# A hybrid decoder layer: narrow products between wide ones, log decays sent as rows, and the order of the key convolutions

## The chip, the core and the metric

The kernel runs on one core of a Trainium2 chip. TensorE (PE in the profile) multiplies, VectorE (DVE), ScalarE (ACT) and GpSimd (POOL) work elementwise, and SyncE (SP) issues all the DMAs. Each engine takes its instructions in the order written for it and waits at semaphores for the others. The metric is device time in microseconds (us), the median over runs, of one launch with batch 1, 1024 tokens and a model width of 1024, all in float32.

## The reference, cut to what matters

The layer is an RMS norm, one input projection, two mixers side by side (a gated delta rule with 4 heads of width 128, and a dilated window attention with 8 heads of width 64), an output projection, and an MLP with a short convolution. The change touches the norm, the gates `b_a`, `a_a`, and the keys of the delta rule:

```
h = rmsnorm(x, norm1_w);  proj = h @ w_in
qkv_a = silu(causal_dwconv(qkv_a, conv_qkv_w))       # width 4, q, k, v of 4 heads
qa = l2norm(qa) * 128 ** -0.5;  ka = l2norm(ka)
beta = sigmoid(b_a)
g = -exp(a_log) * softplus(a_a + dt_bias)            # log decay, one per token and head
gc = cumsum(g over the chunk)
diff = gc[..., :, None] - gc[..., None, :]
dec_incl = where(incl, exp(diff), 0)
lmat = where(strict, dec_incl, 0) * (k @ k^T) * beta
sol = triangular_solve(I + lmat, [v, exp(gc) * k])
```

Then a scan over the chunks, the attention, `x + concat(A, B) @ w_out`, the MLP, and a final norm.

## The kernel before, in words

**Products.** A projection of float32 data is made from three fp32r products of split operands (high by high, low by high, high by low: `mm3`). One such product has 128x128 weights and 512 moving columns; below it is a "wide" product. A column block of the input projection (128 columns of the weights) has two halves of 512 tokens, and each half takes 8 slices of the width x 3 = 24 wide products, collected in one PSUM bank of 512.

**Order of the work.** PE's order is fixed by a planner (class `Weave`): each part of the kernel is a generator that issues products and yields the time until it wants to go on. The planner always lets the ready generator with the lowest level go on, counting time by its own estimates for each engine (`ve`, `ac`, `po_`, `sy`, and the `us` given to `mm`). `norms()` has level 0, `gates()` 1, the key, query and value preparations 3 and 4, `first()` and `dense()` 9, so that wide products fill what the others leave. A token keeps the products on PE in that order. The orders of DVE, ACT, POOL and SP come from a scheduler that runs over dependencies and a cost model of its own; `after()` adds an order without a semaphore.

**Start.** While `xT` arrives in 8 slices, `first()` multiplies each slice with the weights of keys 0 to 2 into six banks (tags `hf`, `asc`, `ch`, two each): 8 x 18 = 144 wide products. Meanwhile `acc` collects the sum of squares. `norms()` reduces `acc` with 8 products of one column (`ones<-acc`), takes the power on POOL, and spreads the result over the partitions by 8 transposes into `rstdB`. `gates()` multiplies the raw slices with an 8 column weight (`xt,wba`, 16 products), turns it back with 8 products of 8 columns (`sel,barow`), computes `g`, and makes the cumulative sum `gc` by one product with a triangle `tri`. These are the narrow products.

**Keys.** `dense()` then runs the column blocks in the order `DENSE`: key 3, two blocks of attention, then q and v by head, and so on. Its two halves alternate in the two `hf` banks. Every bank is emptied by DVE, which multiplies it by `rstdB` into `xr` (`scaled`). `conv_silu` convolves: a copy on ACT, three multiply-adds `d = 1, 2, 3` on DVE, tanh on ACT, and a last multiply-add on DVE. `kprep(h)` then makes from `gc` the decay matrix `dec` of head h: 8 transposes of `gc`, broadcast, into `atr` banks (`ident,gc`), 8 ACT instructions of 128x128 that subtract, a mask on POOL, and an exp on ACT. It transposes the keys (8 products `ident,kT`; ACT copies them to `ktok` and squares them, `sq`, with a sum), multiplies keys by keys (8 products `kT<-kT` into `atr` banks), and DVE scales the result into `um`. The `atr` tag has two banks, so a third user waits until ACT or DVE is done with the first. After the fourth key, `um` goes through DRAM to `forward_sub`, a chain of 62 small DVE instructions, then follow `merge`, the scan `chain`, attention, the output projection and the MLP.

**Slots.** `xr` of key 3 takes a slot of tag `ev`, of which there are two.

```
A("xr", "ev")                       # through scaled(): keys 0, 1 and 3; key 2 takes "qa"
pg = yield from next_bank("atr")    # kprep: bank for the broadcast decays
```

Of the kernel before, what the change touches and what calls it, by code (L numbers as in the profile page):

```python
# [10 lines left out]
OP = mybir.AluOpType  # L11
# [9 lines left out]
FT = 22  # L21
NEG = -1.0e30
EPS = 1e-6
SLOTS = {"kT": 2, "kU": 2, "dv": 2, "dw": 2, "kt": 4, "uy": 5, "qa": 4, "ev": 2, "go": 2, "Xa": 7, "Xb": 9}
# [110 lines left out]
def hybrid_layer(tc, I, out):  # L135
# [35 lines left out]

    def after(inst, anchor):
        tc.add_manual_dep(inst.ins, anchor.ins.name, order, reason="keeps a slot free until it is needed")

# [14 lines left out]
    def split(src, hi, lo):  # L189
        ac.activation(hi, src, AF.Copy)  # L190
        ve.tensor_tensor(lo, src, hi.bitcast(F32), op=OP.subtract)

# [21 lines left out]
    mixer = dp.tile([8, P, S], F32, name="mixer")  # L214
    mdram = dp.tile([H, 32, 1024], F32, name="mdram")
    xdram = dp.tile([H, 32, 1024], F32, name="xdram")
    xtdram = dp.tile([H, 32, 1024], F32, name="xtdram")
# [34 lines left out]
    for k in range(KT):  # L252
# [8 lines left out]
        if k == 0:  # L261
            sy.dma_start(wst[:, 0, :], I["w0"][0, :, 0])
            for h in range(2):
                sy.dma_start(xt[:, half(h)], I["xT"][:P, half(h)])
            sy.dma_start(wst[:, 1, :], I["w0"][0, :, 1])
            split(wst[:, 0, :], whi[:, 0, :], wlo[:, 0, :])
            for h in range(2):
                split_x(xt, 0, half(h))
            split(wst[:, 1, :], whi[:, 1, :], wlo[:, 1, :])
        else:  # L270
            if k % 2 == 0:
                sy.dma_start(wst, I["w0"][k // 2])
            sy.dma_start(xt, I["xT"][k * P:(k + 1) * P, :])
            if k % 2 == 0:
                split(wst, whi, wlo)
            split_x(xt, k, slice(0, S))
        sq = A("sq", "qa")
        ac.activation(sq, xt, AF.Square)
        if k == 0:
            sq0 = sq  # L280
        elif k == 1:
            ve.tensor_tensor(acc, sq0, sq, op=OP.add)
        else:
            ve.tensor_tensor(acc, acc, sq, op=OP.add)

# [41 lines left out]
    def norms():  # L327
        yield wv.need(acc, slack=10.0)
        ssp = yield from next_bank("atr", acc)
        for c in range(NCH):  # L330
            mm(ssp[:, c:c + 1], acc[:, c * P:(c + 1) * P], ones[:, :1], 0.215)
            if c % 2:
                yield 0.4
        ve.tensor_scalar(rst, ssp[:, :NCH], 1.0 / 1024, EPS, op0=OP.mult, op1=OP.add)
# [16 lines left out]
    def gates():  # L351

        yield wv.need(wba, xts[-1], slack=4.0)
        for h in range(2):
            pt = yield from next_bank("atr", wba, xts[-1])
            for k in range(KT):
                o = 32 * (k % 4)
                mm(pt[o:o + 32], wba[:, k, :], xts[k][:, half(h)], 0.3, k < 4, k >= 4, tile_position=(0, o))
            ac.activation(barow[:, half(h)], pt, AF.Copy)
        pt = yield from next_bank("atr", barow)  # L360
        for c in range(NCH):
            mm(pt[:, c * 8:(c + 1) * 8], barow[:, c * P:(c + 1) * P], sel, 0.215)
        yield from wv.until("rst")
        ba = sp.tile([P, NCH, 8], F32, name="ba")
# [17 lines left out]
        pt = yield from next_bank("atr", g)  # L382
        mm(pt[:, :NCH * H], tri, g.rearrange("p c h -> p (c h)"), 0.215)
        ve.tensor_copy(gc, pt[:, :NCH * H].rearrange("p (c h) -> p c h", c=NCH))
# [4 lines left out]

    def scaled(pair, name, by_class=False, tag="ev"):  # L390
        t = A(name, tag)
        for h in range(2):
            sl = half(h)
# [6 lines left out]
        return t  # L400

    def conv_silu(pair, j, name, tag):
        xr = scaled(pair, "xr") if isinstance(pair, list) else pair
        y = A(name, tag)
        ac.activation(y, xr, AF.Copy, scale=gcw[:, j, 3:4])
        for d in (1, 2, 3):
            ve.scalar_tensor_tensor(y[:, d:], xr[:, :S - d], gcw[:, j, 3 - d:4 - d], y[:, d:],
                                           op0=OP.mult, op1=OP.add)
        if j // 4 != 1:
            ac.activation(y, y, AF.Silu)  # L410
            return y

        ac.activation(xr, y, AF.Tanh, scale=0.5)
        ve.scalar_tensor_tensor(y, xr, 1.0, y, op0=OP.add, op1=OP.mult)
        return y
# [22 lines left out]
    def dense():  # L438
# [5 lines left out]
        for i, col in enumerate(DENSE):  # L444
# [51 lines left out]
    def kprep(h):  # L496
# [963 lines left out]
```

## Time and profile before

| | |
|---|---|
| time, median of 3 runs | 1264.93 us (1262.06 to 1266.37) |
| profiled execution: time, span | 1266.99 us, 1265.1 us |
| PE busy | 1241.6 us (98%) |
| DVE, ACT, POOL busy | 940.8, 619.1, 45.0 us |
| mean granted TensorE clock | 0.99 |

The profiled execution's own time is 1.9 us more than its span, which goes from the first to the last instruction. Times inside the trace are counted from the start of the span. PE's records overlap: a wide product is shown with 0.39 us, and the next begins before it ends, so its cost is read from start to start. An idle time in brackets stands just before the instruction, with the engine that ended it.

### The profile page before, as it was taken

How to read it: one execution, taken by the hardware profiler on the slowest of the kernel's cores; microseconds unless marked ns; L12 is line 12 of the kernel's file. 1: busy time of each engine (PE TensorE's matmuls, PEld its weight loads, DVE VectorE, ACT ScalarE, POOL GpSimd, SP SyncE). 2: the span in 40 equal slices, each digit the busy share in tenths (PEclk: the TensorE clock that was granted, in tenths of full speed). 3: DMA queues.
4: the chain of work that ended last, by engine and by line, in shares of the span. 5: the costliest groups of instructions: out<-in, count | busy, mean ns of one | idle time of the engine just before them, and what ended most of it. 6: DMA issues, size and time to landing. Idle time of an engine off the chain costs nothing.

```text
span 1265.1 us, 18365 instructions
## 1 busy us (share of the span) xinstructions
PE 1241.6 (98%) x7070; PEld 1009.2 (80%) x7070; DVE 940.8 (74%) x1466; ACT 619.1 (49%) x1178; POOL 45.0 (4%) x34
## 2 busy tenths in 40 slices
PE   9999999999999999999999999999999999999996
PEld 7878887888676777878888888888888888787886
DVE  7485984573545456666888988988988989899975
ACT  7355544363666375455554444444445444343541
POOL 0012010022000000000000000000000000000000
PEclk9899999999999999999999999999999999999998
DMA  6112243335413321344312123122123198445623
GB/s 225 34 54 57 107 129 106 134 121 198 141 60 106 113 84 43 126 150 150 117 67 100 64 87 100 59 91 100 57 94 100 52 350 305 143 157 193 198 83 134
DMA packets 77767, 151.42 MB, mean 120 GB/s; under 512 B 21744, under 2 KB 28528, under 8 KB 77680
## 3 DMA queue, kind: packets, MB, share of 16 engines
q1 hardware_dynamic: 77680, 150.25, 35.4%
q8 instruction: 55, 0.90, 0.3%
q14 instruction: 32, 0.26, 0.1%
HBM read 112.21 MB, written 35.91 MB: 117 GB/s over the span
## 4 chain that ended last, share of the span: by engine, by line
PE 84%; DVE 6%; DMA 4%; issue 2%; ACT 2%; SPq 1%; POOLq 0%; POOL 0%; DVEq 0%; ACTq 0%
PE ps L176 42%; PE pa L176 19%; PE dw L176 11%; PE pc L176 9%; PE ps L180 4%; DMA wd<-in_wd 1%; DVE pr L131 1%; DVE kT L131 1%; DVE x1h L131 1%; DMA xt<-in_xT 1%; DMA wst<-in_w 1%; SPq L131 1%; DVE wd L131 1%; DMA wst<-in_wu 0%; DVE xr L131 0%
## 5 line engine op out<-in xcount | busy, mean ns | idle before, releaser
L176 PE MATMUL dw<-pr 128*128 128x512 f32 (+1 forms) x984 | 213.7, 377 | 3.2 <-DVE x1h L131 3.0
L176 PEld LDWEIGHTS dw<-pr 128*128 128x128 f32 x984 | 176.0, 188 | 39.8 <-DVE x1h L131 4.9
L176 PE MATMUL ps<-xhi,whi 128*128 128x512 f32 x448 | 188.2, 420 | 2.0 <-DVE xr L131 2.0
L176 PE MATMUL ps<-xhi,wlo 128*128 128x512 f32 x448 | 176.9, 395 | 0.6 <-DVE wlo L131 0.6
L176 PE MATMUL ps<-xlo,whi 128*128 128x512 f32 x448 | 176.6, 394 | 0.0
L176 PE MATMUL pa<-T,pair 128*128 128x512 f32 x528 | 128.7, 393 | 0.8 <-ACT u L131 0.8
L176 PEld LDWEIGHTS pa<-T,pair 128*128 128x128 f32 x528 | 100.1, 190 | 22.1 <-ACT u L131 1.1
L176 PEld LDWEIGHTS ps<-xhi,whi 128*128 128x128 f32 x448 | 85.3, 190 | 21.2 <-issue 5.1
L176 PEld LDWEIGHTS ps<-xhi,wlo 128*128 128x128 f32 x448 | 85.1, 190 | 19.7 <-DVE wlo L131 1.0
L176 PEld LDWEIGHTS ps<-xlo,whi 128*128 128x128 f32 x448 | 85.5, 191 | 13.5
L131 ACT ACTIVATE sm<-sm,mx 128x512 f32<-128x512 f32 (+2 forms) x128 | 79.6, 648 | 23.5 <-DVE mx L131 23.5
L131 ACT ACTIVATE u<-pa 128x512 f32<-128x512 f32 x44 | 26.3, 598 | 110.7 <-PE pa L176 110.7
L131 DVE SCALAR_TENSOR_TENSOR y<-xu,fcw,y 128x1023 f32<-128x1023 f32 (+1 forms) x44 | 56.3, 1281 | 25.7 <-ACT y L131 25.6
L131 ACT ACTIVATE whi<-wst 128x1024 fp32r<-128x1024 f32 (+2 forms) x38 | 38.6, 1017 | 66.1 <-PE ps L176 57.9
L176 PE MATMUL pc<-B,pair 128*128 128x512 f32 x264 | 63.4, 389 | 0.0
L176 PE MATMUL pa<-B,A 128*128 128x512 f32 x264 | 63.4, 389 | 0.0
L176 PE MATMUL pc<-T,S 128*128 128x512 f32 x264 | 63.4, 389 | 0.0
L176 PE MATMUL pa<-T,S 128*128 128x512 f32 x264 | 63.4, 389 | 0.0
L131 DVE TENSOR_TENSOR wst<-wst 128x512 f32<-128x512 f32 x88 | 60.4, 686 | 0.8
L176 PE MATMUL ps<-B,pair 128*128 128x512 f32 x252 | 60.5, 389 | 0.0
L131 ACT ACTIVATE pr<-wd 128x1024 fp32r<-128x1024 f32 x33 | 34.9, 1058 | 50.3 <-DVE wd L131 27.8
L176 PEld LDWEIGHTS pc<-B,pair 128*128 128x128 f32 x264 | 49.5, 188 | 10.3
(229 smaller groups left out, 2286.8 us busy)
## 6 DMA issues: line engine op xcount, KB each, us to landing
wst<-in_wu SPq DMA_DIRECT2D x44, 512.0 KB, 3.6
wd<-in_wd SPq DMA_DIRECT2D x44, 512.0 KB, 3.9
wst<-in_wi SPq DMA_DIRECT2D x25, 512.0 KB, 3.6
upark<-y SPq DMA_DIRECT2D x22, 512.0 KB, 3.5
apark<-aqkv SPq DMA_DIRECT2D x12, 512.0 KB, 2.9
r<-upark SPq DMA_DIRECT2D x11, 512.0 KB, 7.8
r<-upark SPq DMA_DIRECT2D x22, 256.0 KB, 6.7
wa<-in_wd SPq DMA_DIRECT2D x22, 256.0 KB, 2.7
```

What stands on the lines that cost most here:

```text
L131: return getattr(eng, op)(*a, **kw)
L176: tc.stamp_issue_order_token(nc.tensor.matmul(dst, lhs, rhs, start=start, stop=stop, **kw).ins, TOKEN)
L180: tc.stamp_issue_order_token(nc.tensor.transpose(dst, src, ident).ins, TOKEN)
```

## The change

Five edits, all in the first tenth of the run:

1. **Narrow products lie between wide ones.** In `gates()` the planner is made to pause `APART` = 0.5 us after each four `xt,wba` products and after each two `sel,barow` products, and in `norms()` 0.5 in place of 0.4 after each two `ones,acc`. The two waits are set to other slacks, and the estimate of an `xt,wba` product goes from 0.3 to 0.23. The sum of squares of slice 6 is ordered behind the split of the third pair of weights on DVE (`first_lo`).
2. **Log decays as rows.** Beside `tri<-g` a second product makes the same sums with heads and chunks on 32 partitions and tokens along the row. ACT copies it to `grow`, a DMA writes it to `gdram` (16 KB), and for each head a DMA reads 8 rows of 128 values, the same for all 128 partitions, into `dec` (512 KB). The 32 transposes of `gc` go. ACT's 8 subtractions run in place in `dec`.
3. **Order with the rows.** The copy of `gel` is ordered behind the last step of that key's convolution, and the 8 subtractions behind its tanh.
4. **Keys' convolutions in turn.** The second multiply-add of a key is ordered behind the last step of the key before.
5. **The fourth key** scales each half as soon as its bank is full, into a slot of tag `go` in place of `ev`.

```diff
@@ norms, gates
-        yield wv.need(acc, slack=10.0)
+        yield wv.need(acc, slack=8.0)
...
             if c % 2:
-                yield 0.4
+                yield APART
...
-                mm(pt[o:o + 32], wba[:, k, :], xts[k][:, half(h)], 0.3, k < 4, k >= 4, tile_position=(0, o))
+                mm(pt[o:o + 32], wba[:, k, :], xts[k][:, half(h)], 0.23, k < 4, k >= 4, tile_position=(0, o))
+                if k == 3:
+                    yield APART
             ac.activation(barow[:, half(h)], pt, AF.Copy)
+            yield APART
+        yield wv.need(barow, slack=2.0)
...
             mm(pt[:, c * 8:(c + 1) * 8], barow[:, c * P:(c + 1) * P], sel, 0.215)
+            if c % 2:
+                yield APART
...
-        mm(pt[:, :NCH * H], tri, g.rearrange("p c h -> p (c h)"), 0.215)
+        g32 = g.rearrange("p c h -> p (c h)")
+        mm(pt[:, :NCH * H], tri, g32, 0.215)
+        mm(pt[:NCH * H, P:2 * P], g32, tri, 0.215)
+        grow = tile_(sp, [NCH * H, P], F32, "grow", "osq", 1)
+        ac.activation(grow, pt[:NCH * H, P:2 * P], AF.Copy)
+        sy.dma_start(gdram, grow)
@@ sum of squares, slice k
-            ve.tensor_tensor(acc, acc, sq, op=OP.add)
+            inst = ve.tensor_tensor(acc, acc, sq, op=OP.add)
+            if k == 6:
+                after(inst, first_lo, "the products wait for these weights")
@@ conv_silu
+            if j // 4 == 1 and d == 2 and klast:
+                after(inst, klast[-1], "the keys before go first")
...
-        ac.activation(xr, y, AF.Tanh, scale=0.5)
-        ve.scalar_tensor_tensor(y, xr, 1.0, y, op0=OP.add, op1=OP.mult)
+        th = ac.activation(xr, y, AF.Tanh, scale=0.5)
+        klast.append(ve.scalar_tensor_tensor(y, xr, 1.0, y, op0=OP.add, op1=OP.mult))
+        kends[j - 4] = th, klast[-1]
@@ dense
                 pair.append(pt)
+                if kind == "k":
+                    if hh == 0:
+                        xr = A("xr", "go")
+                    scaled(pair, "xr", t=xr, hs=(hh,))
             if kind == "k":
-                T["k", h] = conv_silu(pair, 4 + h, "kT", "kT*")
+                T["k", h] = conv_silu(xr, 4 + h, "kT", "kT*")
@@ kprep
-        for hh in range(2):
-            c0 = 4 * hh
-            pg = yield from next_bank("atr")
-            for c in range(4):
-                tp(pg[:, c * P:(c + 1) * P], gc[:, c0 + c, h:h + 1].to_broadcast([P, P]))
-            pv = pg.rearrange("p (c t) -> p c t", c=4)
-            for c in range(4):
-                ac.activation(v8(dec)[:, c0 + c, :], pv[:, c, :], AF.Identity, bias=ngc[:, c0 + c, h:h + 1])
-            ve.tensor_copy(gel[:, c0:c0 + 4], pv[:, :, P - 1])
+        rows = gdram.rearrange("(c h) t -> h c t", h=H)[h]
+        sy.dma_start(v8(dec), bass.AP(tensor=rows.tensor, offset=rows.offset, ap=[[0, P]] + list(rows.ap)))
+        late = "the rows may come later than the keys"
+        after(ve.tensor_copy(gel, v8(dec)[:, :, P - 1]), kends[h][1], late)
+        for c in range(NCH):
+            inst = ac.activation(v8(dec)[:, c, :], v8(dec)[:, c, :], AF.Identity, bias=ngc[:, c, h:h + 1])
+            after(inst, kends[h][0], late)
```

More of the change, by code (lines that the diff above doesn't have):

```diff
@@ L22 @@
 NEG = -1.0e30
+APART = 0.5
 EPS = 1e-6
@@ L170, in hybrid_layer, with after @@
     order = mybir.DependencyInfo(mybir.DependencyClass.NoSync, mybir.DependencyReason.DATA)
-    def after(inst, anchor):
-        tc.add_manual_dep(inst.ins, anchor.ins.name, order, reason="keeps a slot free until it is needed")
+    def after(inst, anchor, reason="keeps a slot free until it is needed"):
+        tc.add_manual_dep(inst.ins, anchor.ins.name, order, reason=reason)
     def mm(dst, lhs, rhs, us, start=True, stop=True, **kw):
@@ L190, in split @@
         ac.activation(hi, src, AF.Copy)
-        ve.tensor_tensor(lo, src, hi.bitcast(F32), op=OP.subtract)
+        return ve.tensor_tensor(lo, src, hi.bitcast(F32), op=OP.subtract)
     def weight(src, n=1024):
@@ L215, in hybrid_layer @@
     mdram = dp.tile([H, 32, 1024], F32, name="mdram")
+    gdram = dp.tile([NCH * H, P], F32, name="gdram")
     xdram = dp.tile([H, 32, 1024], F32, name="xdram")
@@ L274, in hybrid_layer @@
             if k % 2 == 0:
-                split(wst, whi, wlo)
+                wlast = split(wst, whi, wlo)
             split_x(xt, k, slice(0, S))
@@ L283, in hybrid_layer @@
         else:
-            ve.tensor_tensor(acc, acc, sq, op=OP.add)
+            inst = ve.tensor_tensor(acc, acc, sq, op=OP.add)
+            if k == 6:
+                after(inst, first_lo, "the products wait for these weights")
+        if k == 4:
+            first_lo = wlast
     ident = const("ident", [P, P], I["ident"])
@@ L388, in gates, with scaled @@
         wv.done.add("gates")
-    def scaled(pair, name, by_class=False, tag="ev"):
-        t = A(name, tag)
-        for h in range(2):
+    def scaled(pair, name, by_class=False, tag="ev", t=None, hs=(0, 1)):
+        if t is None:
+            t = A(name, tag)
+        for h in hs:
             sl = half(h)
@@ L400, in scaled @@
         return t
+    klast = []
+    kends = {}
     def conv_silu(pair, j, name, tag):
@@ L406, in conv_silu @@
         for d in (1, 2, 3):
-            ve.scalar_tensor_tensor(y[:, d:], xr[:, :S - d], gcw[:, j, 3 - d:4 - d], y[:, d:],
+            inst = ve.scalar_tensor_tensor(y[:, d:], xr[:, :S - d], gcw[:, j, 3 - d:4 - d], y[:, d:],
                                            op0=OP.mult, op1=OP.add)
+            if j // 4 == 1 and d == 2 and klast:
+                after(inst, klast[-1], "the keys before go first")
         if j // 4 != 1:
```

## The prediction

> **What bounds the kernel now.** I read the page first, then the granted clock in short windows, then PE's timeline with its idle times, then ACT and DVE in the stage of the keys.
>
> ```profile
> span 1265.1 us, 18365 instructions
> PE 1241.6 (98%) x7070; PEld 1009.2 (80%) x7070; DVE 940.8 (74%) x1466; ACT 619.1 (49%) x1178; POOL 45.0 (4%) x34
> PE 84%; DVE 6%; DMA 4%; issue 2%; ACT 2%; SPq 1%; POOLq 0%; POOL 0%; DVEq 0%; ACTq 0%
> ```
>
> PE is busy for 98% and carries 84% of the chain that ended last. What the change can win is PE time in the first 120 us: idle time, slow clock, and products that go. The next rows are windows of 1 us: PE busy (records), granted clock, DMA share, GB/s.
>
> ```profile
> 33.00:34.00 1.00, 0.73 (x7) 1.00 0.78 270
> 34.00:35.00 1.00, 1.00 (x8) 0.64 0.49 197
> 44.00:45.00 1.00, 1.00 (x5) 0.74 0.02 8
> 71.00:72.00 1.00, 0.57 (x2) 0.91 0.00 0
> 75.00:76.00 1.00, 1.00 (x5) 0.88 0.69 184
> ```
>
> A mean of 0.64 between 1.0 and 0.5 means the drop came 0.28 into the us, at 34.28; 0.74 sets its end at 44.52. So PE ran at half clock for 10.24 us. The second drop goes from 71.82 to 75.24, 3.42 us; the first is three times that, so the clock seems to be judged in windows of 3.4 us. PE's timeline shows what came before each drop (start, us, records, idle before):
>
> ```profile
> 25.58 0.50 PE L176 MATMUL ps<-xhi,wlo 128*128 128x512 f32 x1 [0.58 <-DVE wlo L131]
> ...
> 26.70 3.64 PE L176 MATMUL ps<-xt,wba 128*32 128x512 f32 x32
> ...
> 31.79 0.50 PE L176 MATMUL ps<-ones,acc 128*128 128x1 f32 x4
> 33.27 2.68 PE L176 MATMUL ps<-sel,barow 128*128 128x8 f32 x16 [0.98 <-ACT barow L131]
> ...
> 52.04 0.39 PE L176 MATMUL ps<-xhi,whi 128*128 128x512 f32 x1
> ...
> 55.90 0.39 PE L176 MATMUL ps<-xhi,wlo 128*128 128x512 f32 x1
> 56.12 1.03 PE L180 MATMUL ps<-ident,gc 128*128 128x128 f32 x8
> 56.91 0.47 PE L176 MATMUL ps<-xhi,whi 128*128 128x512 f32 x1
> 57.23 0.39 PE L176 MATMUL ps<-xlo,whi 128*128 128x512 f32 x1
> ...
> 68.80 0.65 PE L180 MATMUL ps<-ident,kT 128*128 128x128 f32 x4
> 71.43 0.50 PE L176 MATMUL ps<-xhi,whi 128*128 128x512 f32 x1 [1.97 <-DVE xr L131]
> ...
> 119.17 0.47 PE L176 MATMUL ps<-xhi,whi 128*128 128x512 f32 x1
> ```
>
> From 31.79 to the drop at 34.28 there was 1 us of idle and else only products of 1 and 8 columns; before the second drop PE idled for two of three us, because key 3 could not empty its `hf` banks (DVE was late with its `xr`). A wide product costs 0.227 us at full clock ((55.90 - 52.04) / 17). A block of narrow ones among wide ones adds 0.09: 57.23 - 56.91 is 0.32, not 0.23.
>
> **What goes.**
>
> 1. The split of the third weights comes ahead of a sum on DVE, so the idle time of 0.58 before 25.58 goes: 0.6 us.
> 2. In the new order ten groups of three wide products lie among `wba`, `ones` and `sel`; before `sel` stand, from 26.1 on, 16 `wba` (3.64), 8 `ones` (1.7) and seven groups (4.8), so it comes at 36, well after the `barow` that ended the wait at 33.27. The 0.98 of idle time goes: 1.0 us.
> 3. With wide products on both sides of each pair of narrow ones (0.42 us a pair: 7 records in 0.73, two to a product, 0.21 each) the emptiest 3.4 us hold about 63% of streaming products, against some 25% before the first drop. A stretch of the scan, 5 us of products of 128 columns (46 records, two to a product, so 0.22 each), kept the full clock:
>
> ```profile
> 257.00:262.00 5.00, 5.00 (x46) 1.00 0.22 74
> ```
>
> So narrow products without a gap need not drop it, and I take it that the clock stays: 10.24 x 0.5 = 5.1 us. Against this, four more blocks at 0.09 and the second `tri` product, at most one narrow product, 0.2: -0.6. Idle between narrow products is not proven harmless, so the bounds are 0 and 5.1.
> 4. The 32 `gc` transposes: 57.23 - 0.23 - 56.12 = 0.88 for eight. Two blocks of eight and four of four at half of that: 3.5 us.
> 5. The fourth key: `xr` gets a slot that is free long before, and each half is scaled when its bank is full. By DVE's order both halves are out before the next column block needs the bank. 1.97 idle and 3.42 x 0.5 of clock: 3.7 us.
>
> Together 13.3 us.
>
> **What comes instead.** PE takes its products in order. The new order puts key 0's products with itself 18 wide products behind the end of key 3's block (before: 24, with the 2 us wait and the half clock besides), and all four keys into 120 wide products (before 147). ACT's queue does not shrink: each key keeps its 8 subtractions, 8 squares, 2 copies and an exp. ACT and DVE, start and us:
>
> ```profile
> 66.17 2.16 ACT L131 ACTIVATE dec<-ps,ngc 128x128 f32<-128x128 f32 x8
> 68.17 1.10 ACT L131 ACTIVATE xr<-kT 128x1024 f32<-128x1024 f32 x1
> 69.12 1.10 ACT L131 ACTIVATE whi<-wst 128x1024 fp32r<-128x1024 f32 x1
> 70.07 1.10 ACT L131 ACTIVATE dec<-dec 128x1024 f32<-128x1024 f32 x1
> ...
> 75.12 0.28 ACT L131 ACTIVATE sq<-ps 128x128 f32<-128x128 f32 x1
> 75.53 0.28 ACT L131 ACTIVATE sq<-ps 128x128 f32<-128x128 f32 x1
> 65.08 2.46 DVE L131 SCALAR_TENSOR_TENSOR kT<-xr,gcw,kT 128x1021 f32<-128x1021 f32 x2
> 81.87 2.15 DVE L131 SCALAR_TENSOR_TENSOR um<-ps,bp,dec 128x128 f32<-128x128 f32 x8
> ```
>
> From start to start: 1024 columns on ACT 0.95, eight subtractions 2.0 (taken for SBUF too; bounds 1.6 and 2.2), a square 0.41, a copy of 512 taken as half of 0.95; on DVE a multiply-add 1.2 and a last step the same, four `um` 1.05. Let U be the end of key 3's block. Key 0's transposes lie just ahead of U, and ACT is through with their two copies at U + 0.4. Then stand on ACT, by its new order: a weight split, tanh of key 1, the convolution copy of key 3, a square, key 0's exp, a square, key 1's eight subtractions, a small one, and the square that frees the bank: 4 x 0.95 + 3 x 0.41 + 2.0 + 0.1 = 7.1, with hand-overs U + 8.0. PE is there at U + 4.1 (18 x 0.227). **It waits 3.9 us.** The second four need the bank freed behind 3 more squares, two small ones, key 3's tanh and key 1's exp: U + 11.7, against U + 10.35 (0.88 for the first four and their bank change, 6 x 0.227, 0.09): 1.35. Key 1's transposes need `um` of key 0. On DVE that stands, from the end of key 3's tanh at U + 9.9, behind three steps of 1.2, an `aqkv` half (counted 1.0) and small ones of 0.8, and takes 1.05: U + 16.3 against 15.4: 0.9. The same chain gives 0.9 and 0.3 later. Sum 7.4 (bounds 3 and 10, from the hand-overs and the subtractions). A wait of 3.9 takes the clock down for 3.4 us, 1.7 of PE time, but the 1.35 above is then hidden: +0.5. After the keys, DVE's multiply-adds of q stand behind the first step of `forward_sub`, which waits for a load:
>
> ```profile
> 120.04 1.12 DVE L131 SCALAR_TENSOR_TENSOR um<-ps,bp,dec 128x128 f32<-128x128 f32 x4
> 129.62 0.19 DVE L131 TENSOR_TENSOR tmp<-mt,xi 128x31 f32<-128x31 f32 x1 [2.31 <-DMA mt<-mdram]
> ```
>
> 8.5 us from the last `um` to that step; I count 0.5 for q's transposes. `forward_sub` itself begins earlier than it did against PE, so later products get no worse wait. Loss 8.4.
>
> The rows of `gdram`: SP issues the write and four loads behind two weight loads that went long before, ahead of one that waits for a slot until U. The windows above show the DMA engines idle at 44 and 71 (0.02 and 0.00). DMA rows: packets, MB and share in a stretch of 14 us (184 to 198) full of 128 B rows; a 512 KB load's time to landing.
>
> ```profile
> q1 hardware_dynamic: 8211, 1.51, 62.9%
> mt<-mdram SPq DMA_DIRECT2D x1, 512.0 KB, 4.2
> ```
>
> 8211 packets took 0.629 x 16 x 14 = 141 us of engine time, 17 ns each. A head has 1024 pieces of 512 B; between one and four such packets each, that is 1.1 to 4.4 us over 16 engines. The `tri` product stands 18 wide ones behind the last `sel`, near 46; with 4.2 at most for the write and for the first load the rows are there at 54, the fourth by 68. ACT wants key 0's after its tanh: six `xr` halves at half of 1.2 and five multiply-adds on DVE behind a bank full near 47.5, then 0.95, so near 58; the last after 75. So the loads are hidden by 4 us, at no cost.
>
> **Sum.** 13.3 - 8.4 = 4.9 us. The profiled execution took 1266.99, 1.9 over its span; it would take 1262. It lies 2.1 above the median of 1264.93, so the median goes to 1260.
>
> **Rivals.**
>
> - *No wait on ACT* (subtractions from SBUF are quicker, or the last products come later): up to all of 13.3, 1251.6 to 1256. For it: ACT's work in the stage, 4 x (2.0 + 3.3 + 0.95 + 0.95) and eight of 0.95, is 36 us, no more than PE's 38 (120 x 0.227, 8 x 0.44, and 8 x 0.88 for the keys' own products, counted like eight transposes). Against: the order, not the amount, makes the first wait. Chance 0.25.
> - *The clock is not what the spreading changes.* If pairs of narrow products among wide ones still drop it, or if it dropped by phase alone, 5.1 goes and the time is 1265, no change. For it: pairs of `ones` lay between groups of three already in the second half of the first drop, and did not end it. Chance 0.10. [...]
> - *Slower: the half clock outlasts the wait.* After the 3.9 us wait each 3.4 us window holds another wait of about 1 us. If that is enough to keep the clock down, each window costs 1.7. It hides 3.5 us of the waits, so (4.9 + 3.5 + 0.5) / 1.7, five windows, eat the gain; eight, to the end of the keys near 97 us, give 1270. Against: the second drop before ended after one window with a block of transposes in it. Chance 0.08.
> - *The rows come late.* Each load at 10 us and not 4.4: `dec` of key 3 at 70 and of key 2 at 90 hold ACT, PE waits 10 more, 1270. Chance 0.05.
>
> **Numbers.** The forecast has 0.52; its own range is 1257 to 1262.5, from the bounds of the waits. A measurement tells about 0.3%, 3.8 us, from no change, so it gives 0.37 to faster, 0.13 to no change, 0.02 to slower. With the rivals (0.25 faster; 0.10 no change; 0.13 slower): 0.62, 0.23, 0.15. The range 1252 to 1266 leaves 0.06 below and 0.13 above.
>
> **What would show it.** Right: no half clock from 34 to 45; the next column block begins without idle time behind key 3; a wait of about 4 us at key 0's own products, some 66 us in, ended by ACT's `sq`, and a drop of clock right after; wide product 336 (119.17 before) at 112 to 114; `dec` loads landed by 67. Wrong: no idle time of over 1 us there (then 1252), or clock 0.5 in 34 to 45 or from 70 on, or ACT idle before the subtractions for a DMA.

## The result, and the profile after

The changed kernel takes 1257.9 us (median; 1257.1 to 1259.56) where the kernel before takes 1265.18 beside it on the same chip: ratio 0.9946, 95% interval 0.9932 to 0.9959. Measured a second time, beside other kernels, it took 1259.23 against 1264.08, ratio 0.9965 (0.9952 to 0.9978). So it is faster by 0.35 to 0.54%, 4.4 to 6.8 us. The prediction was 1260, 4.9 less than before.

The profiled execution took 1259.56 us. Three lines of its page, for those shown of before:

```profile
span 1257.8 us, 18320 instructions
PE 1233.0 (98%) x7040; PEld 1002.1 (80%) x7040; DVE 936.0 (74%) x1462; ACT 621.8 (49%) x1179; POOL 47.8 (4%) x34
PE 84%; DVE 7%; DMA 4%; ACT 2%; issue 2%; SPq 0%; POOL 0%; POOLq 0%; DVEq 0%; ACTq 0%
```

PE is busy for 98% as before; 8.6 us of busy time have gone (1241.6 - 1233.0), of which half clock is a part. Windows of 1 us of the changed kernel (PE busy, granted clock, DMA share, GB/s):

```profile
34.00:35.00 1.00, 1.00 (x7) 1.00 0.51 184
44.00:45.00 1.00, 1.00 (x6) 1.00 0.00 0
70.00:71.00 1.00, 0.00 (x0) 0.61 0.00 0
71.00:72.00 1.00, 0.65 (x3) 0.50 0.00 0
76.00:77.00 1.00, 1.00 (x6) 0.50 0.00 0
77.00:78.00 1.00, 1.00 (x8) 0.97 0.00 0
```

The half clock from 34 to 45 is gone. A new one goes from 70.22 (0.61 in the first row: 0.22 of it at 1.0) to 77.06: 6.84 us, two windows of 3.42, where the prediction had one. PE's timeline of the changed kernel shows what it follows (start, us, records, idle before):

```profile
38.80 0.65 PE L181 MATMUL ps<-ident,rst 128*128 128x128 f32 x4 [0.78 <-DVE rstdB L132]
...
61.12 1.03 PE L181 MATMUL ps<-ident,kT 128*128 128x128 f32 x8
...
71.35 2.07 PE L177 MATMUL ps<-kT 128*128 128x128 f32 x8 [4.42 <-ACT sq L132]
...
75.78 1.66 PE L177 MATMUL ps<-kT 128*128 128x128 f32 x8
...
87.19 1.16 PE L177 MATMUL ps<-kT 128*128 128x128 f32 x8 [0.57 <-ACT sq L132]
...
113.72 0.39 PE L177 MATMUL ps<-xhi,whi 128*128 128x512 f32 x1
```

Key 0's own products wait 4.42 us for the square that frees their bank (predicted 3.9). The second four come without a wait. The wide product 336 starts at 113.72 (119.17 before; predicted 112 to 114). All 1344 wide products of the projection are in both traces, in the same order, so the same product's start can be compared in any two kernels; against product 24, which lies ahead of all edits and begins at other times in other executions (12.72 here, 13.12 in the changed kernel's second profile, 13.51 before), the gain at 336 is 4.66 us. This is the figure used below, "the gain at 336", since it is read to a tenth of a us, where medians are not. And ACT's timeline of the changed kernel:

```profile
57.89 1.06 ACT L132 ACTIVATE xr<-kT 128x1024 f32<-128x1024 f32 x1 [3.68 <-DVE kT L132]
60.33 2.46 ACT L132 ACTIVATE dec<-dec,ngc 128x128 f32<-128x128 f32 x8 [1.38 <-DVE gel L132]
62.69 0.19 ACT L132 ACTIVATE ge<-gel 128x8 f32<-128x8 f32 x1
...
64.10 1.05 ACT L132 ACTIVATE whi<-wst 128x1024 fp32r<-128x1024 f32 x1
...
68.49 2.46 ACT L132 ACTIVATE dec<-dec,ngc 128x128 f32<-128x128 f32 x8
70.83 0.22 ACT L132 ACTIVATE ge<-gel 128x8 f32<-128x8 f32 x1
```

ACT stands idle for 3.68 and 1.38 us ahead of key 0's subtractions, before the tanh and behind it, and the wait on PE ends just after key 1's. The second idle time, 1.38, ends with the copy of `gel`: it has to read `dec` before the subtractions overwrite it in place, and edit 3 orders it behind key 0's last step. No wait of ACT in this stage is ended by a DMA.

### The profile page after: what moved, and what is told of

The parts are those of the page before. It is cut to its first block, busy times and chain, and to the rows that moved or that the text cites. A ratio compares the mean times of both kernels' runs of the same rounds, so it can differ in the third digit from the quotient of the medians.

```text
span 1257.8 us, 18320 instructions
## 1 busy us (share of the span) xinstructions
PE 1233.0 (98%) x7040; PEld 1002.1 (80%) x7040; DVE 936.0 (74%) x1462; ACT 621.8 (49%) x1179; POOL 47.8 (4%) x34
## 4 chain that ended last, share of the span: by engine, by line
PE 84%; DVE 7%; DMA 4%; ACT 2%; issue 2%; SPq 0%; POOL 0%; POOLq 0%; DVEq 0%; ACTq 0%
PE ps L177 44%; PE pa L177 18%; PE pc L177 9%; PE dw L177 8%; PE ps L181 4%; DMA wd<-in_wd 3%; DVE pr L132 2%; DVE x1h L132 1%; DVE wd L132 1%; ACT dec L132 1%; DVE kT L132 1%; PE warm L177 1%; DMA wst<-in_wu 0%; DVE r L132 0%; DVE xr L132 0%
```

## Experiments

Gains at 336 are against the kernel before (119.17, its product 24 at 13.51).

| kernel | median us | ratio to before | gain at 336 |
|---|---|---|---|
| changed kernel | 1257.9, again 1259.23 | 0.9946, again 0.9965 | 4.66, again 4.60 |
| e1, spreading alone | 1258.41 | 0.9959 (0.9943 to 0.9975) | 6.41 |
| e2, changed, decays by transposes | 1256.36 | 0.9936 (0.9921 to 0.9952) | 7.99 |
| e3, changed, key 3 in `ev` | 1259.73 | 0.9962 (0.9947 to 0.9978) | 3.77 |
| e4, changed, keys not in turn | 1262.71 | 0.9989 (0.9978 to 0.9999) | 1.57 |
| e5, key 0's subtractions early | 1256.17 | 0.9938 (0.9922 to 0.9954) | 6.88 |
| e6, wait filled | 1259.02 | 0.9961 (0.9947 to 0.9976) | 5.23 |
| e7, products later | 1261.6 | 0.9981 (0.9971 to 0.9991) | 3.33 |
| e8, narrow together | 1258.42 | 0.9957 (0.9940 to 0.9974) | 6.07 |
| e9, subtraction on POOL | 1259.41 | 0.9970 (0.9958 to 0.9982) | 4.03 |
| e10, e2 and e8 together | 1254.81 | 0.9932 (0.9914 to 0.9950) | 9.69 |
| e12, e10 with rows for two keys | 1254.56 | 0.9930 (0.9918 to 0.9943) | 7.38 |

e11 is the changed kernel again.

### e1: the spreading alone

The kernel before, with edit 1 only:

```diff
+            if k == 6:
+                after(inst, first_lo, "the products wait for these weights")
...
-                yield 0.4
+                yield APART
...
+                if k == 3:
+                    yield APART
...
+        yield wv.need(barow, slack=2.0)
...
+            if c % 2:
+                yield APART
```

> The kernel before with the first part of the change alone: norm and gate products spread among the wide ones, the third weights' split ahead of the sum. Theory (the half clock from 34 to 45 comes from narrow products that stand together with 1 us of idle time): no window under 1.00 from 20 to 60 us, idle before barow and wlo gone, the new 0.8 us wait for rstdB there; 10.24 x 0.5 + 1.6 - 0.4 - 0.8 = 5.5 us less than 1265.2, 1259.7; the drop at 72 with key 3's 2 us idle stays. Rival (the clock drops there by phase, whatever the products): half clock stays somewhere in 30 to 50, about 1264.5.

Ratio 0.9959, 5.2 us, close to the theory's 5.5, and no half clock before 600. But the second drop was expected to stay, and it went too, though key 3's idle time is there as before. PE in e1, and the edges of a later drop in e1's windows:

```profile
66.44 0.50 PE L177 MATMUL ps<-xhi,whi 128*128 128x512 f32 x1 [1.97 <-DVE xr L132]
```

```profile
617.00:618.00 1.00, 0.40 (x3) 0.86 0.00 0
621.00:622.00 1.00, 1.00 (x6) 0.93 0.00 0
```

The kernel before has such a late drop too:

```profile
624.00:625.00 1.00, 0.86 (x3) 0.89 0.00 0
628.00:629.00 1.00, 1.00 (x7) 0.90 0.28 33
```

In before the three drops begin at 34.28, 71.82 and 624.78: 37.54 us apart is 11 times 3.413, and 552.96 is 162 times 3.413. So within one execution the drops lie on a grid of 3.413 us. The other kernels' drops agree: in e9 the first and the late one begin at 63.50 and 619.88, 163 such intervals apart, and in e3, e4, e7 and e8 161, 164, 158 and 160. In before the idle time of 1.97 us (69.46 to 71.43) lies whole in one interval of the grid, 68.41 to 71.82, and the drop follows at its end. In e1 the grid goes through 617.72 and so, 162 intervals earlier, through 64.8: the idle time (64.47 to 66.44) is cut there, 0.3 in one interval and 1.7 in the next, and no drop follows. One and the same stall was followed by 3.42 us of half clock in before and by none in e1, and the phase of the grid is what differs there. Half clock is counted as half of PE's time, so this is an estimated 1.7 us or nothing; in before wide products begin 0.43 us apart at half clock (42.34 to 44.05 for four), 0.227 at full clock. Of e1's gain at 336, 6.41, 1.7 is this luck; 4.7 is edit 1. The changed kernel's gain is 4.66, so edits 2 to 5 together brought nothing by then.

### e2: decays by transposes again

```diff
-        rows = gdram.rearrange("(c h) t -> h c t", h=H)[h]
-        sy.dma_start(v8(dec), bass.AP(...))
...
+        for hh in range(2):
+            pg = yield from next_bank("atr")
+            for c in range(4):
+                tp(pg[:, c * P:(c + 1) * P], gc[:, c0 + c, h:h + 1].to_broadcast([P, P]))
...
```

> The changed kernel with the decays spread by PE transposes again, all else kept. Theory: 32 transposes of 0.11 come back, PE has no other idle time for them, and the subtractions read PSUM (2.0 and not 2.4 us for eight): 3.5 more, 0.4 less wait, 1261. Rival: PE waits at key 0's products anyway, and ACT's subtractions, which no longer stand behind a load and a tanh, come earlier in its queue, so that the wait of 4.4 us and its two windows of half clock shrink by as much as the transposes cost: 1257 to 1258, no difference.

The rival's side, and more: 32 transposes more on PE, and the gain at 336 is 7.99, 3.3 more than the changed kernel's. There is no wait before key 0's products, though they stand 21 wide products behind key 0's first transposes in both kernels, and no half clock before 600. Key 0's products and product 336 on PE in e2, then ACT:

```profile
70.77 1.16 PE L177 MATMUL ps<-kT 128*128 128x128 f32 x8
...
110.63 0.47 PE L177 MATMUL ps<-xhi,whi 128*128 128x512 f32 x1
```

```profile
51.43 2.17 ACT L132 ACTIVATE dec<-ps,ngc 128x128 f32<-128x128 f32 x8
53.44 1.20 ACT L132 ACTIVATE kT<-xr,gcw 128x1024 f32<-128x1024 f32 x1
...
59.81 2.17 ACT L132 ACTIVATE dec<-ps,ngc 128x128 f32<-128x128 f32 x8
...
64.25 1.06 ACT L132 ACTIVATE xr<-kT 128x1024 f32<-128x1024 f32 x1 [2.26 <-DVE kT L132]
```

Here the subtractions of keys 0 and 1 are done by 62, between stretches in which ACT is idle (2.26 in the last row). In the changed kernel the same work starts at 60.33 and 68.49. So 3.5 us of transposes were paid for with some 7 us of waiting and slow clock. One thing more differs: in e2 the planner puts key 0's transposes and products 9 wide products later (198 and 219, not 189 and 210) and the keys' last products at 336, not 309, which may leave ACT more room. e2 alone doesn't tell this from the place of the subtractions on ACT; e5 and e7 below bear on it.

### e3: key 3 in the `ev` slot again

```diff
-                if kind == "k":
-                    if hh == 0:
-                        xr = A("xr", "go")
-                    scaled(pair, "xr", t=xr, hs=(hh,))
...
-                T["k", h] = conv_silu(xr, 4 + h, "kT", "kT*")
+                T["k", h] = conv_silu(pair, 4 + h, "kT", "kT*")
```

> The changed kernel with key 3's banks scaled into the ev slot again, both halves at the end. Theory (two independent stalls): 1.97 us idle before the first A block returns, and the wait at key 0's products stays at 4.4 us: 2 us of idle time more, half clock earlier and no shorter, 1260 to 1261.6. Rival (one backlog on ACT and DVE: a stall ahead of key 0's products is taken out of the wait behind it): idle at the bank 2 us, wait at sq 2.4 us or less, 1257.5 to 1258.5.

```profile
71.84 2.08 PE L177 MATMUL ps<-kT 128*128 128x128 f32 x8 [6.42 <-ACT sq L132]
```

Neither came as written. No idle time stands at the bank; the planner put key 0's products 9 wide ones earlier (201, not 210), which is 2.0 us, and the wait grew by 2.0, to the same moment (71.84 for 71.35, 0.4 of it from the start of the run). The gain at 336 fell by 0.9; the ratio, 0.9962, doesn't tell from the changed kernel. That PE goes on at the same moment wherever its products stand is the rival's picture of one backlog; that a stall ahead would be taken out of the wait isn't shown, since none stood there. Nor did key 3's idle time need edit 5 to go: here it stays away without it.

### e4: the keys not in turn

```diff
-            if j // 4 == 1 and d == 2 and klast:
-                after(inst, klast[-1], "the keys before go first")
```

> The changed kernel without the orders that put the keys' convolutions in turn; PE's order is the same. Theory: key 0's last step stands behind two more multiply-adds of DVE (2.4 us), its transposes at 61 us wait up to 2 us and everything ACT does behind them comes as much later: 1259.5 to 1261. Rival: the wait at key 0's products comes from ACT's queue alone, which starts with the loads, so the time is 1258, no difference, or the clock drop only moves.

```profile
63.57 1.53 PE L181 MATMUL ps<-ident,kT 128*128 128x128 f32 x8 [1.97 <-DVE gel L132]
...
75.71 2.08 PE L177 MATMUL ps<-kT 128*128 128x128 f32 x8 [4.66 <-ACT sq L132]
```

The theory's mechanism, 2 us at the transposes, but dearer than said: the wait at the products stays as it was behind it, and half clock stands in three intervals. The gain at 336 falls to 1.57. With the subtractions tied to the keys' ends, edit 4 carries 3 us.

### e5: key 0's subtractions not held back

```diff
-        after(ve.tensor_copy(gel, v8(dec)[:, :, P - 1]), kends[h][1], late)
+        inst = ve.tensor_copy(gel, v8(dec)[:, :, P - 1])
+        if h > 0:
+            after(inst, kends[h][1], late)
...
-            after(inst, kends[h][0], late)
+            if h > 0:
+                after(inst, kends[h][0], late)
```

> The changed kernel with the order taken off key 0 alone that puts its last-column copy and its eight subtractions behind its own convolution; PE's order is the same. Theory (the wait of 4.4 us comes from that order, which holds eight subtractions back on an ACT that sits idle for 3.7 us before 58, while the rows land from 52 on): key 0's subtractions run before 58, the first bank comes free near 67.5, the wait falls under 1 us, the second four may wait up to 2, no half clock from 70 to 77: 4 to 6 us less than the changed kernel, ratio to before 0.990 to 0.992, 1252 to 1254. Rival (the rows come too late to be used earlier, and DVE or ACT stands for the load): DVE's column copy waits for the load and holds the keys, wait unchanged or longer: 1257 to 1260.

DVE and PE in e5:

```profile
54.62 0.17 DVE L132 COPY gel<-dec 128x8 f32<-128x8 f32 x1 [1.07 <-DMA dec<-gdram]
```

```profile
62.97 1.06 PE L181 MATMUL ps<-ident,kT 128*128 128x128 f32 x8 [1.16 <-DVE kT L132]
...
72.62 1.16 PE L177 MATMUL ps<-kT 128*128 128x128 f32 x8 [1.33 <-ACT sq L132]
...
88.44 1.16 PE L177 MATMUL ps<-kT 128*128 128x128 f32 x8 [1.45 <-ACT sq L132]
```

Both were right in part. The wait of 4.4 us goes, and with it every half clock; but DVE's copy now waits 1.07 for the load, which puts key 0 and its transposes 1.2 later, and smaller waits follow (1.33, 0.81, 1.45). Together they come to 4.75, where the changed kernel waits 4.99, so what was won is mainly the clock. Gain at 336 6.88, 2.2 more than the changed kernel; the ratio, 0.9938, lies below both of the changed kernel's, but its interval overlaps theirs, and 1256.17 us misses the theory's 1252 to 1254. The order was a cause of the long wait, since PE's order is the same in both; without it the first row, which landed at 54.6, is itself 1 us late.

### e6: the wait filled with products

```diff
+            if h == 0 and c0 == 0:
+                fill = bank("asc")
+                for _ in range(19):
+                    mm(fill[:, :P], ident, ident, 0.0)
```

> The changed kernel with 19 products of 128 columns into a bank that nobody reads, put just ahead of key 0's own products (19 x 0.22 = 4.2 us of the 4.4 us wait): it prices the clock without the wait. Theory (the idle time takes the clock down): granted clock 1.00 from 70 to 77, 3.4 us of PE time back, some 1 to 2.5 of it lost to later waits that the half clock covered: 1255 to 1257, ratio 0.993 to 0.9935. Rival (something else takes the clock down there, or the drop costs nothing as it only covers waits): 1258, ratio 0.9945 or more.

```profile
67.25 4.41 PE L177 MATMUL ps<-ident 128*128 128x128 f32 x38
71.79 1.16 PE L177 MATMUL ps<-kT 128*128 128x128 f32 x8
...
75.00 1.16 PE L177 MATMUL ps<-kT 128*128 128x128 f32 x8 [0.67 <-ACT sq L132]
...
79.91 0.66 PE L181 MATMUL ps<-ident,kT 128*128 128x128 f32 x4 [1.02 <-DVE um L132]
```

The granted clock is 1.00 in the windows of 1 us from 70 to 73 and at 76, where it was 0.50 to 0.61 in the changed kernel: with the idle time the half clock went too. But the half clock had cost PE an estimated (6.84 - 1.13) / 2 = 2.9 us, as PE stood for 1.13 of it, and only 0.6 of that comes back (gain at 336 5.23, was 4.66): waits of 0.67, 1.02 and 0.56 stand where the half clock and a wait of 0.57 stood, and the scheduler ordered ACT's later work a little otherwise. The median, 1259.0, shows nothing of it and misses the theory's 1255 to 1257: on the price the rival is right. In this run PE is not the bound from 67 to 90, and the slow clock there was nearly free; e5, with nearly the same sum of waits and no half clock, gained 2.2, so it is not free in every order.

### e7: key 0's products later

```diff
-            pt = yield from next_bank("atr")
+            if h == 0 and c0:
+                yield 5.5
+            pt = yield from next_bank("atr", slack=0.0 if h or c0 else 4.2)
...
+        if h == 1:
+            yield from wv.until(("kk", 0))
```

> The changed kernel with key 0's own products moved back on PE by 21 and 30 wide products (4.8 and 6.8 us), key 1's transposes behind them. Theory (the wait is only a matter of the order on PE): wide products fill the wait, no half clock at 70, wide product 336 at 107 to 109, 1250 to 1254, ratio 0.989 to 0.9915. Rival (ACT and DVE are behind by as much for all keys, so the wait returns at key 1's transposes or products): idle of 2 to 4 us before 95, 1256 to 1259.

```profile
82.84 1.12 PE L181 MATMUL ps<-ident,kT 128*128 128x128 f32 x4 [5.67 <-DVE um L132]
```

The rival: no wait at key 0's products, but 5.67 us at key 1's transposes, for the bank that `um` of key 0 empties, and two intervals of half clock from 81.04. The gain at 336 falls to 3.33, and 1261.6 us is slower than the rival's 1256 to 1259 too. Placed like this, the products move the wait and don't shorten it, which speaks for a bound in the chain over ACT and DVE.

### e8: narrow products together

The changed kernel without the pauses, but with the planned wait for `barow`:

```diff
             if c % 2:
-                yield APART
...
-                if k == 3:
-                    yield APART
             ac.activation(barow[:, half(h)], pt, AF.Copy)
-            yield APART
         yield wv.need(barow, slack=2.0)
```

> The changed kernel with the norm and gate products together again (16 wba, 8 ones, 8 sel, each in one block with 3 and 6 wide ones between), but with no idle time before barow, since the wait for it is planned. Theory A (narrow products themselves take the clock down): a half clock between 33 and 45 of 3.4 to 10.2 us, 1.7 to 5 us slower than the changed kernel, ratio 0.996 to 0.9985. Theory B (idle time decides, narrow products only in that they leave the window emptier): granted clock 1.00 from 25 to 60, ratio 0.994 to 0.995, as the changed kernel.

```profile
35.60 0.65 PE L181 MATMUL ps<-ident,rst 128*128 128x128 f32 x4 [0.40 <-POOL rst L132]
```

As theory B: no half clock before 71, and at wide product 168 it is 1.4 us ahead of the changed kernel (ahead of before by 6.70 and 5.31, product 24 taken off): fewer blocks, and a wait of 0.40 in place of 0.78. The ratio, 0.9957, lies between the two theories and doesn't decide. e12, with the same first stage, shows below that this was one of two outcomes.

### e9: the subtraction on POOL

```diff
-        for c in range(NCH):
-            inst = ac.activation(v8(dec)[:, c, :], v8(dec)[:, c, :], AF.Identity, bias=ngc[:, c, h:h + 1])
-            after(inst, kends[h][0], late)
+        po_.tensor_copy(gel, v8(dec)[:, :, P - 1])
+        po_.tensor_tensor(v8(dec), v8(dec), gc[:, :, h:h + 1].to_broadcast([P, NCH, P]), op=OP.subtract)
...
+        after(ve.tensor_tensor(gend, gel, gc[:, :, h], op=OP.subtract), kends[h][1], late)
+        after(ac.activation(dec, dec, AF.Exp), kends[h][0], late)
```

The planner also counts a square 0.18 us dearer, which puts key 0's own products 6 wide products earlier (204, not 210).

> The changed kernel with the subtractions and the last-column copies on POOL, one instruction of 1024 columns a key in place of ACT's eight, and squares counted 0.18 us dearer when the products are placed (key 0's own products 6 and 15 wide ones behind the bank change, which was 21 and 27). Theory (the stage of the keys is bound by ACT's and DVE's queues, not by PE; four times 2.4 us taken off ACT shorten it): POOL, idle there, does a subtraction in 1 to 2.5 us before 58; key 0's bank comes free near 68, wait 2 us or less in spite of the earlier place, sum of the waits from 60 to 115 under 3 us, wide product 336 at 107 to 110.5 from a start as in the changed kernel; ratio 0.9885 to 0.992, 1250 to 1254. Rival 1 (DVE's chain of multiply-adds and um bounds it): waits move to um, gain under 2 us. Rival 2 (POOL's subtraction slows DVE or takes over 4 us): key 0's exp waits for it, no gain, 1258 or more.

DVE in the changed kernel, the same two instructions in e9, and POOL in e9:

```profile
58.98 1.23 DVE L132 SCALAR_TENSOR_TENSOR kT<-xr,kT 128x1024 f32<-128x1024 f32 x1 [0.59 <-ACT xr L132]
...
61.40 0.17 DVE L132 TENSOR_TENSOR gend<-gel,gc 128x8 f32<-128x8 f32 x1
```

```profile
60.86 2.73 DVE L132 SCALAR_TENSOR_TENSOR kT<-xr,kT 128x1024 f32<-128x1024 f32 x1 [0.59 <-ACT xr L132]
63.52 1.05 DVE L132 TENSOR_TENSOR gend<-gel,gc 128x8 f32<-128x8 f32 x1
```

```profile
58.49 2.14 POOL L132 TENSOR_SCALAR_AFFINE_SELECT dec<-dec 128x1024 f32<-128x1024 f32 x1
60.60 1.91 POOL L132 TENSOR_TENSOR dec<-dec,gc 128x1024 f32<-128x1024 f32 x1
62.59 1.96 POOL L132 TENSOR_SCALAR_AFFINE_SELECT dec<-dec 128x1024 f32<-128x1024 f32 x1
```

Rival 2. While POOL works on SBUF, DVE's steps take 2.73 us for 1.23 and 1.05 for 0.17, and POOL's mask takes 2.14 where it took 1.10 in the changed kernel: in these rows each is slower beside the other. DVE's last step, begun at 60.86, ends at 63.59, 1.1 us after POOL's subtraction has ended (60.60 + 1.91 = 62.51), as if it had run only then. Key 0 came 2.2 us late, half clock followed (63.50 to 66.92), and the gain at 336 is 4.03. Why they are slower isn't shown; the traces give the durations alone.

### e10: transposes, and narrow products together

> Decays by PE transposes again as in e2, and the norm and gate products together again as in e8 (with the planned wait for barow): of the change only the planned barow wait, the split ahead of the sum, the keys in turn and key 3's slot are left. Theory (idle time, not narrowness, takes the clock down, and the rows by DMA cost more than they bring): no half clock before 600, wide product 336 at 110 as in e2, ratio 0.993 to 0.994, as e2. Rival (the spreading is needed, e8 was luck of the window's phase): a half clock between 30 and 45, ratio 0.996 to 0.998.

The edits are those of e2 and e8. As the theory: no half clock before 1244, gain at 336 9.69, 5 us more than the changed kernel's, with product 336 at 108.86. Ratio 0.9932, 1254.81 us.

### e11 and e12: the changed kernel again, and rows for keys 2 and 3 only

> The changed kernel as it is, beside the next one on one chip, to compare ratios and to see what of its first profile comes back. By all theories ratio 0.9945, 1257 to 1258.5; wait of 4.4 us ended by sq and two windows of half clock behind it again; the half clock at 617 to 628, which its first profile did not have and most others had, may come back, 1.7 us.

The wait (4.38), the two intervals of half clock (71.02 to 77.86) and the gain at 336 (4.60) came back; the late drop did not come. Ratio 0.9965, not the 0.9945 that was expected.

```diff
+        if h < 2:
+            for hh in range(2):
+                pg = yield from next_bank("atr")
...
+        else:
             rows = gdram.rearrange("(c h) t -> h c t", h=H)[h]
```

> As e10, but only keys 0 and 1 spread their decays by PE transposes; keys 3 and 2, whose transposes came at 270 to 315 wide products, take the rows by DMA. Theory (rows by DMA cost only where the subtractions must wait behind the key while ACT is idle before and backed up after; ACT's idle stretches of 3 to 5 us in e10 at 81 to 99 take the later keys' subtractions): 16 transposes of 0.11 less than e10, waits under 1.5 us, wide product 336 at 107 to 108.5, ratio 0.990 to 0.9925. Rival (any subtraction tied to the key's tanh backs ACT up, whichever the key): a wait of 2 us or more at the products of keys 1 to 3, ratio 0.994 to 0.996.

PE and windows of e12:

```profile
33.07 1.84 PE L177 MATMUL ps<-sel,barow 128*128 128x8 f32 x16
35.32 0.65 PE L181 MATMUL ps<-ident,rst 128*128 128x128 f32 x4 [0.40 <-POOL rst L132]
...
87.91 1.16 PE L177 MATMUL ps<-kT 128*128 128x128 f32 x8 [1.33 <-ACT sq L132]
```

```profile
36.00:37.00 1.00, 1.00 (x6) 0.73 0.40 156
39.00:40.00 1.00, 1.00 (x4) 0.56 0.06 16
```

Between the two. The waits come to 2.5 us (1.33, 0.74, 0.44), not under 1.5, and take back the 16 transposes: from product 168 to 336 e12 gains 3.1 us on the kernel before, e10 3.2. So rows gain nothing for the later keys either. And with the first stage of e8 and e10 the clock did drop, from 36.46 to 39.88: here all eight `sel` products, the wait of 0.40 and four transposes lie in one interval of the grid (33.05 to 36.46). Narrow products together dropped the clock in one of three profiles, spread in none of ten. The ratio is 0.9930 (0.9918 to 0.9943) against 0.9965 for the changed kernel beside it on one chip: e12 is faster than both kernels. e10, with 0.9932 at another time, can't be told from it by time; by the gain at 336 it is 2.3 ahead, 1.7 of which is e12's half clock.

## Why the prediction was right, and where it was not

**The spreading (1.6 of idle time, 5.1 of clock, 0.6 back).** Right. The waits for `wlo` and `barow` and the half clock are gone. Three things were missed. The second four `rst` transposes wait 0.78 for DVE's `rstdB`, which nothing in the sum had. And at wide product 168 the gain is 5.31, where the terms up to there, 8 of the transposes (0.88) among them, make 7.0: 0.8 is that wait, and 0.9 is left. For the split blocks the sum had 4 x 0.09; e8 puts them at 1.0 (1.4 less the difference of the waits), which is 0.6 of the 0.9. Most of the rest is the second `tri` product, counted 0.2:

```profile
46.14 0.30 PE L177 MATMUL ps<-g,tri 128*128 128x32 f32 x2
46.37 0.41 PE L177 MATMUL ps<-tri,g 128*32 128x128 f32 x2
46.71 0.50 PE L177 MATMUL ps<-xhi,whi 128*128 128x512 f32 x1
```

The next wide product starts 0.57 us behind `ps<-g,tri` here and 0.14 behind it before (49.05 to 49.19), so the second product cost 0.4. The working also had the emptiest 3.4 us at 63% of streaming products. The interval of the grid from 36.1 to 39.5 (ten ahead of the drop at 70.22) has 0.78 us of idle time, some `sel` products, all eight `rst` transposes and no more than three wide products, and the clock stayed at 1.0: that it held there was not reasoned out, and by what margin isn't shown.

**The transposes (3.5) and key 3 (1.97 and 1.7).** They are gone, and so is the idle time at `hf`. But e2 shows that the transposes were no gain, since what took their place cost more; e1 that the 1.7 of clock hangs on the phase of the grid; and e3 that edit 5, which was given both, was not needed for the idle time to go. Edit 5 is worth 0.9 at 336.

**The wait on ACT.** Right in place and nearly in size: 66.93, ended by `sq`, 4.42 for 3.9. The items counted from the weight split to the square that frees the bank stand on ACT in that very order, and take 7.1 us as summed (64.10 to 71.18): key 1's subtractions took 2.3 for 2.0, the three squares 0.25 for 0.41 each. What was off is their start. The end of key 3's block, U, is 62.69 here, and ACT was through with key 0's copies at U + 1.4, not U + 0.4, because key 0's own subtractions ran only from 60.33 to 62.69 and the copies stood behind them. Smaller hand-overs (0.2 for 0.5) took back some of it. The price of a subtraction was outside its bounds: in place in SBUF eight take 2.36 from start to start, where the prediction took 2.0 with an upper bound of 2.2; from PSUM they take 2.01 (51.43 to 53.44 in e2). That is 0.295 and 0.251 us for one.

One reason given for the wait fell. The prediction compared 18 wide products of distance behind key 3's block with 24 before. Counted from key 0's first transposes, which is where ACT's work on the bank begins, the changed kernel and e2 both have 21, and e2 has no wait. A cause of the long wait is that edit 3 holds key 0's subtractions back past 5 us in which ACT is idle (3.68 and 1.38): without that order, and with the same order on PE, e5 waits 1.33 there, behind transposes that come 1.2 later. How much of e2's freedom from waits is due to the room that the planner gave it on PE stays open.

**The later waits and the clock.** 1.35, 0.9, 0.9 and 0.3 were counted, and 0.5 for one interval of half clock. There were 0.57 of waiting and two intervals: 1.13 us of the wait (70.22 to 71.35) reached into the first of them, and the next stayed at half clock. The parts were wrong and the sum held: 4.42 + 0.57 + 2.9 = 7.9, predicted 7.4 + 0.5 (the working's 1.7 less 1.35 is 0.35, not 0.5). That is partly luck; e6 shows waits and half clock standing for each other, but not to the tenth.

**Rows and q.** The first row landed at 54.6 in e5, where DVE waited for it, and at 54.0 in the changed kernel, which issues its load 0.5 us earlier (predicted 54). ACT waited for no DMA. q's transposes wait not at all (0.5 predicted).

**The rest.** At 336 the working gives 13.3 - 7.9 = 5.4, measured 4.66. From there on the prediction expected nothing but 0.5 for q. In the first profile 0.8 came ahead of product 24, and 1.0 more by product 1248 (500.51 and 494.07), while idle time between 115 and 510 us fell from 3.4 to 2.1; the late half clock of before (624.78 to 628.20), worth 1.7, isn't in the changed kernel's two profiles, though it is in 7 of the other 11. None of this is among the prediction's terms, so 6.8 us in the first measurement owes something to luck. Why the second gave 4.4 isn't shown: its profile lacks the late half clock too, and gains 1.1 us between products 336 and 1248, where the first gains 1.0.

Of the rivals, *no wait on ACT* is wrong, *the half clock outlasts the wait* came in small (one interval more, and by e6 nearly free), and *the rows come late* is wrong. *The clock is not what the spreading changes* is wrong for edit 1 as a whole; but in e8 and e10 the planned wait for `barow` was enough without the spreading, in e12 it was not, and with the spreading none of ten profiles dropped there.

Two of the prediction's own marks don't hold up. Half clock from 70 on was to be a sign of being wrong, and it came, but the same list expects a drop right behind a wait that ends near 70, so this sign can't tell. And the narrower range, 1257 to 1262.5, doesn't follow from the bounds of the waits: waits of 3 in all, with the 0.5 of clock and the 0.5 of q, give 13.3 - 4.0 = 9.3 us, 1255.6.

Not settled: which of edits 2 to 4 keeps key 3's idle time away, why e7's `um` came as late as it did, and how much of e9's loss is due to the earlier place of the products.

## What to carry to other kernels

Of five edits put in together, one had the whole gain, and only running it alone showed that. Work taken from the busiest engine was worth nothing where another engine's queue set the pace: ask what stands in that queue, and never order work behind an event that comes later than the engine's last idle time. A transfer that is hidden can still cost, through the order that was written to keep anybody from waiting for it. To compare two versions in which PE does the same products, compare the start of one and the same product; here it resolved tenths of a us where medians resolved two.

## What the runs showed of the hardware

- In one execution the drops of the granted clock lie on a grid of 3.413 us (11 and 162 intervals between the drops of before). Its phase differs between executions of one kernel: in the changed kernel's two profiles the drop begins 57.50 and 57.90 us behind the start of product 24 (70.22 - 12.72, 71.02 - 13.12).
- 1.97 us idle within one interval was followed by a drop (before, and e4 from 64.02 on); the same 1.97 cut into 0.3 and 1.7 was not (e1), nor was 1.88 beside wide products (e8, in the interval 64.70 to 68.11, where a wait of 4.26 begins). After an interval at half clock with 1.13 us idle the clock stayed at half for the next (changed kernel, 70.22 to 77.06).
- Eight products of 8 columns, 0.40 us idle and four of 128 columns in one interval, with three wide ones, were followed by a drop (e12, 33.05 to 36.46, then half clock to 39.88). In e10 most of the `sel` products, a wait of 0.22, seven transposes and three wide products in one interval were not.
- With POOL at work on SBUF beside it, a step of DVE took 2.73 us for 1.23 and another 1.05 for 0.17, and POOL's mask took 2.14 for 1.10 (e9, against the changed kernel).
- A subtraction of 128 columns on ACT took 0.295 us from SBUF (changed kernel, 2.36 for eight) and 0.251 from PSUM (e2, 2.01 for eight).
